# Three products of the RWKV-7 chain summed in one PSUM bank, with VectorE copying an operand out

## The chip, the core and the metric

The kernel runs on one core of a Trainium2 chip. The metric is the device time of one launch in microseconds (us), as a median of runs; lower is better. TensorE (PE) multiplies matrices into the eight banks of PSUM, VectorE (DVE) and ScalarE (ACT) read PSUM and SBUF, GpSimd (POOL) works on SBUF, and SyncE (SP) issues most transfers. Each of these takes its instructions strictly in the order in which they stand in its own queue.

## What is computed

One decoder layer over 1024 tokens of width 1024, in float32: an RMS norm, one wide input projection, three branches (RWKV-7 time mixing, a convolution module, cross-attention into 256 memory tokens), a gated merge, an output projection and a final norm. The change lies in the RWKV-7 branch. Its recurrence and the group norm behind it, cut from the reference:

```python
def step(state, inp):                       # per head; state is 64 x 64, all in float32
    r_t, w_t, k_t, v_t, a_t, b_t = inp
    sa = jnp.einsum('bhvk,bhk->bhv', state, a_t)
    state = (state * w_t[:, :, None, :]
             + sa[..., :, None] * b_t[:, :, None, :]
             + v_t[..., :, None] * k_t[:, :, None, :])
    y = jnp.einsum('bhvk,bhk->bhv', state, r_t)
    return state, y
_, ys = lax.scan(step, s0, seqs)            # 1024 steps, 16 heads
...
mu = jnp.mean(wkv, axis=-1, keepdims=True)
var = jnp.mean(jnp.square(wkv - mu), axis=-1, keepdims=True)
wkv = ((wkv - mu) * lax.rsqrt(var + RWKV_GN_EPS)).reshape(B, S, RWKV_WIDTH)
```

## The kernel before

**Stages.** Up to some 100 us the input is normalized and transposed. Up to some 1035 us the recurrence of the 16 heads runs between the matmuls of the input projection, and the rest of the time goes to the convolution, the attention and the output projections. Each float32 weight tile is split into two rounded parts, `wh` and `wl` (ACT casts, L123, DVE subtracts, L124), and each product of the projection is three matmuls of 128x512 into a bank `d` (L298, called dense matmuls here). 24 dense matmuls fill one bank.

**The chain.** A feature tile `j` (0 to 7) holds two heads, and the tokens come in two halves `e` (0 and 1). For each of these 16 pairs `g_chain` handles 8 chunks of 64 tokens in two groups `q` of 4, one chunk after the other, since each needs the state S that the one before left. The state of the two heads is a 128x128 tile, `s0[0]` and `s0[1]` in turn. `g` holds the masked products of all token pairs in a chunk, and `TT` the inverse of a triangular matrix that `g_sub` computes by substitution (31 steps of two small DVE instructions, L587 and L590, on tiles `W` and `U`).

- `g_pre` prepares a group: it transposes the keys into `tk` and the values into `sav`, multiplies `TT` into `tk` and `g`, and multiplies the part of `g` called AK with the values V (L666). AK V lands in the second half of a bank `tr` and ACT copies it to `Y` (L675).
- For each chunk PE multiplies `ar` by the state into a bank `ry` (L709). Half of the 128 rows of the result are the A S that the new operand needs, the other half are R S, a part of the output. DVE adds A S and the AK V in `Y` into `sav` (L710). PE multiplies `tk` by `sav` into a bank `sas` (L717), and two DVE instructions (L720), one for each head, turn that and ACT's scaled copy of the state (L713) into the next state.
- After four chunks PE multiplies `g` by `sav` into a bank `tr` (L731), ACT copies that to `Y` (L733), and two DVE instructions add the R S rows of `ry` (L738). Then come the statistics of the group norm (L742).
- After eight chunks, the tail of the chain: small DVE instructions, a reciprocal root on POOL (L114, L118), two DVE instructions over all of `Y` (L760, L761), and PE transposes `Y` into a bank `tr` (L766). DVE turns that into `o`, which SP stores to `o_rwkv_d` (L771).

**Banks.** PSUM's eight banks are `d` (2), `g` (2), `ry` (2), `sas` (1) and `tr` (1). The one bank `tr` serves the transposes of `g_pre`, AK V, the two products of `g_sub` that finish `TT` (L615 and L625, with ACT's copies `zt` and `TT` between, L619 and L629), the product of L731 and the transposes of the tail. Each user waits until the one before has been read.

**What sets the order.** The generators for dense work, `g_prep` (which makes `g`, `ar`, `bk`), `g_sub` and `g_chain` are mixed by shares of a step count in `mix`. From that the Tile framework's scheduler draws each engine's order, by its own estimates and by which banks and buffers are free in them, so an edit of the banks can move instructions on all engines. The order repeats with a period of one `j`, some 115 us: a chain for `e`=0, then one for `e`=1. Their two tails are called **tail 0** and **tail 1** here.

Of the kernel before, what the change touches and what calls it, by code (L numbers as in the profile page):

```python
# [13 lines left out]
ALU = mybir.AluOpType  # L14
# [4 lines left out]
P = 128  # L19
# [5 lines left out]
C = 64  # L25
# [7 lines left out]
RMS_EPS = 1e-6  # L33
LN_EPS = 1e-5
GN_EPS = 64e-5
PAIR_EVERY = 34.0
TAP = 1.4
LOS = (13, 14, 15, 16, 17)
# [24 lines left out]
def hybrid_kernel(ctx: ExitStack, tc: tile.TileContext, x: bass.AP, mem: bass.AP, wt: bass.AP,  # L63
# [272 lines left out]
    with tc.tile_pool(name="rk", bufs=1, reuse_waits="tile") as rk:  # L336
# [53 lines left out]
        def fl(ap):  # L390
            return ap.rearrange("p a t -> p (a t)")
# [240 lines left out]

        state = [0]

        def g_pre(j, e, q, g, bk, v, Y):
            tkp = bank("tr")
            for cc in range(4):
                pe.transpose(tkp[:, cc * P:(cc + 1) * P], fl(bk[:, q * 4 + cc, :, :]), ident)  # L640
            tk = rk.tile([P, 4, P], F32, name="tk", tag="tk", bufs=2)
            act.copy(tk, tkp.rearrange("p (c t) -> p c t", t=P))
            yield
            vtp = bank("tr")
            for cc in range(2):
                c = q * 4 + cc * 2
                pe.transpose(vtp[:, cc * P:(cc + 1) * P], v[:, c * C:(c + 2) * C], ident)
            sav = rk.tile([P, 4, P], F32, name="sav", tag="sav", bufs=2)
            for par in range(2):
                rows = slice(ko(par), ko(par) + C)  # L650
                act.copy(sav[rows, par::2, :], vtp[rows, 0:2 * P].rearrange("p (c t) -> p c t", t=P))
            yield
            zv = vtp[:, 2 * P:4 * P]
            u1 = bank("g", 2)
            uv = u1.rearrange("p (k c h t) -> p k c h t", k=2, c=2, h=2)
            for n in range(4):
                cc2, hh = n // 2, n % 2
                vsl = slice(hh * C, (hh + 1) * C)
                for par in range(2):
                    own = slice(so(par), so(par) + C)  # L660
                    oth = slice(ko(par), ko(par) + C)
                    cc = cc2 * 2 + par
                    gc = g[:, par, hh, q * 2 + cc2]
                    pe.matmul(uv[own, 0, cc2, hh, :], lhsT=TT[own, hh * 4 + q * 2 + cc2, :], rhs=tk[own, cc, vsl],
                              start=True, stop=True)
                    pe.matmul(zv[own, n * C:(n + 1) * C], lhsT=gc[oth, own], rhs=sav[oth, cc, vsl],  # L666
                              start=True, stop=True)
            for n in range(4):
                cc2, hh = n // 2, n % 2
                for par in range(2):  # L670
                    own = slice(so(par), so(par) + C)
                    oth = slice(ko(par), ko(par) + C)
                    pe.matmul(uv[own, 1, cc2, hh, :], lhsT=TT[own, hh * 4 + q * 2 + cc2, :],
                              rhs=g[own, par, hh, q * 2 + cc2, oth], start=True, stop=True)
            act.copy(fl(Y[:, q * 2:q * 2 + 2, :]), zv)  # L675
            for par in range(2):
                own = slice(so(par), so(par) + C)
                oth = slice(ko(par), ko(par) + C)
                act.copy(tk[own, par::2, :], uv[own, 0].rearrange("p c h t -> p c (h t)"))
                act.copy(g[own, par, :, q * 2:q * 2 + 2, oth], uv[own, 1].rearrange("p c h t -> p h c t"))  # L680
            yield (tk, sav)

        def g_chain(j, e):
            g, ar, bk, pc = GG.pop((j, e)), AR.pop((j, e)), BK.pop((j, e)), PCS.pop((j, e))
            v = VS.pop((j, e))
            if e == 0:
                dve.memset(s0[state[0]], 0.0)

            Y = rk.tile([P, 4, P], F32, name="Y", tag="Y", bufs=1)
            st = rk.tile([P, 4, 2, 6], F32, name="st", tag="st", bufs=1)  # L690
            pre = [g_pre(j, e, q, g, bk, v, Y) for q in range(2)]
            got = None
            for got in pre[0]:
                yield
# [2 lines left out]
            bv = rk.tile([P, HS], F32, name="bv", tag="bv", bufs=1)  # L697
            dve.tensor_tensor(out=bv, in0=bp, in1=v, op=ALU.mult)
            for q in range(2):
                tk, sav = got  # L700
                ry = bank("ry", 2)
                for cc in range(4):
                    c = q * 4 + cc
                    par = c % 2
                    cg = e * CPH + c
                    own = slice(so(par), so(par) + C)
                    cs = slice(cc * P, (cc + 1) * P)
                    S0, S1 = s0[state[0]], s0[1 - state[0]]
                    pe.matmul(ry[:, cs], lhsT=fl(ar[:, c, :, :]), rhs=S0, start=True, stop=True)  # L709
                    dve.tensor_tensor(out=sav[own, cc, :], in0=ry[own, cs], in1=Y[own, c // 2, :], op=ALU.add)  # L710
                    if cg < NCH - 1:
                        sp = rk.tile([P, P], F32, name="sp", tag="sp", bufs=1)
                        act.activation(sp, S0, AF.Copy, scale=pc[:, c:c + 1])  # L713
                    yield
                    if cg < NCH - 1:
                        sn = bank("sas")
                        pe.matmul(sn[:, 0:P], lhsT=tk[:, cc, :], rhs=sav[:, cc, :], start=True, stop=True)  # L717
                        for hh in range(2):
                            vsl = slice(hh * C, (hh + 1) * C)
                            dve.scalar_tensor_tensor(out=S1[vsl, vsl], in0=sn[vsl, vsl], scalar=pc[vsl, c:c + 1],  # L720
                                                     in1=sp[vsl, vsl], op0=ALU.mult, op1=ALU.add)
                        state[0] = 1 - state[0]
                    if q == 0 and cc < 3:
                        got = next(pre[1])
                    yield
                yp = bank("tr")
                for n in range(4):
                    cc2, hh = n // 2, n % 2
                    for par in range(2):
                        oth = slice(ko(par), ko(par) + C)  # L730
                        pe.matmul(yp[oth, n * C:(n + 1) * C], lhsT=g[:, par, hh, q * 2 + cc2, oth],  # L731
                                  rhs=sav[:, cc2 * 2 + par, hh * C:(hh + 1) * C], start=True, stop=True)
                act.copy(fl(Y[:, q * 2:q * 2 + 2, :]), yp[:, 0:2 * P])  # L733
                yield
                ryv = ry.rearrange("p (c t) -> p c t", t=P)
                for par in range(2):
                    oth = slice(ko(par), ko(par) + C)
                    dve.tensor_tensor(out=Y[oth, q * 2:q * 2 + 2, :], in0=Y[oth, q * 2:q * 2 + 2, :],  # L738
                                      in1=ryv[oth, par::2, :], op=ALU.add)
                for c2 in range(q * 2, q * 2 + 2):  # L740
                    for hh in range(2):
                        dve.bn_stats(out=st[:, c2, hh, :], in_=Y[:, c2, hh * C:(hh + 1) * C])  # L742
                yield
# [511 lines left out]
```

## Time and profile before

| what | value |
|---|---|
| median of 3 runs | 1951.31 us (1950.67 to 1953.14) |
| the profiled execution's own time | 1949.77 us |
| its span in the trace | 1947.8 us |
| PE busy over the span | 1844.5 us (95%) |
| DVE busy | 1410.6 us (72%) |
| ACT busy | 691.9 us (36%) |
| POOL busy | 227.7 us (12%) |
| mean granted TensorE clock | 0.993 of full speed |

PE is busy for 95% of the span, and the matmuls' number does not depend on the order, so the time is PE's work and PE's waits. "Busy" counts modelled ends of overlapping matmuls; a wait can thus be a little longer than the idle time that a row gives in brackets. The profile names for each idle stretch what released it. A wait of another engine matters where PE then waits for it.

### The profile page before, as it was taken

How to read it: one execution, taken by the hardware profiler on the slowest of the kernel's cores; microseconds unless marked ns; L12 is line 12 of the kernel's file. 1: busy time of each engine (PE TensorE's matmuls, PEld its weight loads, DVE VectorE, ACT ScalarE, POOL GpSimd, SP SyncE). 2: the span in 40 equal slices, each digit the busy share in tenths (PEclk: the TensorE clock that was granted, in tenths of full speed). 3: DMA queues.
4: the chain of work that ended last, by engine and by line, in shares of the span. 5: the costliest groups of instructions: out<-in, count | busy, mean ns of one | idle time of the engine just before them, and what ended most of it. 6: DMA issues, size and time to landing. Idle time of an engine off the chain costs nothing.

```text
span 1947.8 us, 30024 instructions
## 1 busy us (share of the span) xinstructions
PE 1844.5 (95%) x11412; PEld 1472.2 (76%) x11412; DVE 1410.6 (72%) x3028; ACT 691.9 (36%) x1303; POOL 227.7 (12%) x311
## 2 busy tenths in 40 slices
PE   6999998999899898998999999999999999899998
PEld 5777776766676676776788888888888788778886
DVE  5667787777878777787735998898999857654423
ACT  6334343433344343343333323131313335432121
POOL 2201111111111112111000000000000223100001
PEclk9999999999999999999999999999999999999999
DMA  4232212222121222212224411112122666785432
GB/s 147 57 99 58 77 35 63 60 56 74 42 83 44 62 63 53 77 42 71 69 72 141 130 54 55 65 59 71 44 76 87 227 199 214 246 283 170 129 130 86
DMA packets 127936, 188.61 MB, mean 97 GB/s; under 512 B 64432, under 2 KB 66608, under 8 KB 127792
## 3 DMA queue, kind: packets, MB, share of 16 engines
q1 hardware_dynamic: 122704, 178.11, 29.8%
q10 hardware_dynamic: 4768, 8.07, 1.1%
q8 instruction: 89, 1.46, 0.3%
q0 software_dynamic: 320, 0.52, 0.1%
q14 instruction: 55, 0.45, 0.1%
HBM read 139.92 MB, written 46.20 MB: 96 GB/s over the span
## 4 chain that ended last, share of the span: by engine, by line
PE 63%; DVE 23%; DMA 4%; issue 4%; ACT 3%; POOL 3%; SPq 0%; DVEq 0%; POOLq 0%; ACTq 0%
PE d L298 41%; PE g L298 5%; PE g L212 4%; DVE W L590 3%; DVE tm L587 3%; PE d L212 2%; DVE s L720 2%; PE g L552 2%; DVE wl L124 2%; DVE sav L710 1%; PE ry L894 1%; POOL vr L118 1%; DVE Y L761 1%; DVE Y L738 1%; PE sas L717 1%
## 5 line engine op out<-in xcount | busy, mean ns | idle before, releaser
L298 PE MATMUL d<-hH,wh 128*128 128x512 f32 x1504 | 607.2, 404 | 2.4 <-ACT lc L383 2.0
L298 PE MATMUL d<-hH,wl 128*128 128x512 f32 x1504 | 603.0, 401 | 0.0
L298 PE MATMUL d<-hL,wh 128*128 128x512 f32 x1504 | 600.1, 399 | 0.0
L298 PEld LDWEIGHTS d<-hH,wl 128*128 128x128 f32 x1504 | 285.0, 189 | 56.9
L298 PEld LDWEIGHTS d<-hH,wh 128*128 128x128 f32 x1504 | 285.3, 190 | 55.8 <-ACT lc L383 2.4
L298 PEld LDWEIGHTS d<-hL,wh 128*128 128x128 f32 x1504 | 285.0, 189 | 53.6
L848 DVE SCALAR_TENSOR_TENSOR ac<-up,wdw,ac 128x1024 f32<-128x1024 f32 x240 | 308.0, 1283 | 11.8 <-ACT ac L845 5.9
L123 ACT CAST wh<-wf 128x1024 fp32r<-128x1024 f32 x137 | 143.6, 1049 | 311.3 <-PE d L298 277.1
L124 DVE TENSOR_TENSOR wl<-wf,wh 128x1024 fp32r<-128x1024 f32 x137 | 177.6, 1296 | 83.8 <-ACT wh L123 83.3
L590 DVE TENSOR_TENSOR W<-W,tm 128x60 f32<-128x60 f32 (+24 forms) x496 | 112.3, 226 | 10.0
L587 DVE TENSOR_TENSOR tm<-W,U 128x60 f32<-128x60 f32 (+24 forms) x496 | 107.7, 217 | 11.1
L713 ACT ACTIVATE sp<-s,pc 128x128 f32<-128x128 f32 x120 | 48.3, 402 | 174.8 <-DVE s L720 137.6
L717 PEld LDWEIGHTS sas<-sav,tk 128*128 128x128 f32 x240 | 38.5, 188 | 67.7 <-DVE sav L710 49.4
L717 PE MATMUL sas<-sav,tk 128*128 128x128 f32 x240 | 54.2, 307 | 34.3 <-DVE sav L710 32.6
L720 DVE SCALAR_TENSOR_TENSOR s<-sas,pc,sp 64x64 f32<-64x64 f32 x240 | 67.6, 282 | 21.5 <-PE sas L717 16.1
L298 PE MATMUL g<-oH,wh 128*128 128x512 f32 x192 | 76.3, 398 | 5.3 <-ACT wh L123 5.3
L298 PE MATMUL g<-oH,wl 128*128 128x512 f32 x192 | 76.2, 397 | 2.1 <-DVE wl L124 2.1
L298 PE MATMUL g<-oL,wh 128*128 128x512 f32 x192 | 75.8, 395 | 0.0
L298 PE MATMUL d<-oL,wh 128*128 128x512 f32 x192 | 75.2, 392 | 0.0
L298 PE MATMUL d<-oH,wl 128*128 128x512 f32 x192 | 75.2, 392 | 0.0
L298 PE MATMUL d<-oH,wh 128*128 128x512 f32 x192 | 75.2, 392 | 0.0
L710 DVE TENSOR_TENSOR sav<-ry,Y 64x128 f32<-64x128 f32 x128 | 36.8, 287 | 43.7 <-ACT Y L675 26.8
(301 smaller groups left out, 2910.6 us busy)
## 6 DMA issues: line engine op xcount, KB each, us to landing
wf<-in_wt_dram SPq DMA_DIRECT2D x137, 512.0 KB
g_d<-gt SPq DMA_DIRECT2D x48, 256.0 KB
U<-ud SPq DMA_DIRECT2D x64, 128.0 KB
nxt<-in_x_dram SPq DMA_DIRECT2D x8, 512.0 KB
o_rwkv_d<-o SPq DMA_DIRECT2D x16, 256.0 KB
cv_d<-ac SPq DMA_DIRECT2D x8, 512.0 KB
o_mem_d<-om SPq DMA_DIRECT2D x16, 256.0 KB
xs<-cv_d SPq DMA_DIRECT2D x8, 512.0 KB
```

The costliest lines, as they stand in the source:

```text
L123: act.copy(hi, src)
L124: (eng or dve).tensor_tensor(out=lo, in0=src, in1=hi.bitcast(F32), op=ALU.subtract)
L212: pe.matmul(po, lhsT=l, rhs=r, start=(i == 0), stop=(i == n - 1))
L298: pe.matmul(po, lhsT=l[:, ks_], rhs=r[:, k, sl], start=(n == 0), stop=(n == 3 * KT - 1))
L552: pe.matmul(gps[hh][:, cc * P:(cc + 1) * P], lhsT=fl(bk[rows, c, :, :]), rhs=fl(ar[rows, c, :, :]), start=True, stop=True)
L587: dve.tensor_tensor(out=tv, in0=W[:, 0:m, i:i + 1].broadcast_to([NG * 32, m, n]), in1=U[:, i:i + 1, i + 1:32].broadcast_to([NG * 32, m, n] ...
L590: dve.tensor_tensor(out=wv_, in0=wv_, in1=tv, op=ALU.add)
L710: dve.tensor_tensor(out=sav[own, cc, :], in0=ry[own, cs], in1=Y[own, c // 2, :], op=ALU.add)
L713: act.activation(sp, S0, AF.Copy, scale=pc[:, c:c + 1])
L717: pe.matmul(sn[:, 0:P], lhsT=tk[:, cc, :], rhs=sav[:, cc, :], start=True, stop=True)
L720: dve.scalar_tensor_tensor(out=S1[vsl, vsl], in0=sn[vsl, vsl], scalar=pc[vsl, c:c + 1], in1=sp[vsl, vsl], op0=ALU.mult, op1=ALU.add)
L848: dve.scalar_tensor_tensor(out=ac, in0=up[:, tap:tap + S], scalar=wdw[:, tap * 8 + j:tap * 8 + j + 1], in1=ac, op0=ALU.mult, op1=ALU.add)
```

## The change

AK V is no longer written to a bank `tr` and copied to `Y`. Its matmuls write the `ry` bank of the group, which is now taken in `g_pre`; the first of them for each half of the rows starts the sums. The matmul of `ar` by the state adds to that (`start=False`), so that the rows of A S hold A S + AK V, and DVE copies them to `sav` with `tensor_copy` in place of the add. The product of `g` by `sav` is added onto the R S rows of the same bank, and two ACT copies of 64 rows take the sum to `Y`, in place of one ACT copy of 128 rows and two DVE adds. The manual dependencies only fix PE's own order. Nothing else is edited; the numbers of instructions on PE, ACT, POOL and SP stay the same, and DVE has 64 fewer. Cut to its core:

```diff
@@ g_pre
-            zv = vtp[:, 2 * P:4 * P]
+
+            ry = bank("ry", 2)
+            first = {}
             u1 = bank("g", 2)
...
-                    pe.matmul(zv[own, n * C:(n + 1) * C], lhsT=gc[oth, own], rhs=sav[oth, cc, vsl],
-                              start=True, stop=True)
+
+                    mm = pe.matmul(ry[own, cc * P + hh * C:cc * P + (hh + 1) * C], lhsT=gc[oth, own],
+                                   rhs=sav[oth, cc, vsl], start=par not in first, stop=False,
+                                   skip_group_check=True)
+                    if par in first:
+                        tc.add_manual_dep(mm.ins, first[par].name, NOSYNC, reason="sums begun in order")
+                    else:
+                        first[par] = mm.ins
...
-            act.copy(fl(Y[:, q * 2:q * 2 + 2, :]), zv)
...
-            yield (tk, sav)
+            yield (tk, sav, ry, first)
@@ g_chain
-                tk, sav = got
-                ry = bank("ry", 2)
+                tk, sav, ry, first = got
...
-                    pe.matmul(ry[:, cs], lhsT=fl(ar[:, c, :, :]), rhs=S0, start=True, stop=True)
-                    dve.tensor_tensor(out=sav[own, cc, :], in0=ry[own, cs], in1=Y[own, c // 2, :], op=ALU.add)
+                    mm = pe.matmul(ry[:, cs], lhsT=fl(ar[:, c, :, :]), rhs=S0, start=False, stop=False,
+                                   skip_group_check=True)
+                    for begun in first.values():
+                        tc.add_manual_dep(mm.ins, begun.name, NOSYNC, reason="sums begun in order")
+                    dve.tensor_copy(sav[own, cc, :], ry[own, cs])
...
-                yp = bank("tr")
                 for n in range(4):
                     cc2, hh = n // 2, n % 2
                     for par in range(2):
                         oth = slice(ko(par), ko(par) + C)
-                        pe.matmul(yp[oth, n * C:(n + 1) * C], lhsT=g[:, par, hh, q * 2 + cc2, oth],
-                                  rhs=sav[:, cc2 * 2 + par, hh * C:(hh + 1) * C], start=True, stop=True)
-                act.copy(fl(Y[:, q * 2:q * 2 + 2, :]), yp[:, 0:2 * P])
+                        cc = cc2 * 2 + par
+                        pe.matmul(ry[oth, cc * P + hh * C:cc * P + (hh + 1) * C],
+                                  lhsT=g[:, par, hh, q * 2 + cc2, oth], rhs=sav[:, cc, hh * C:(hh + 1) * C],
+                                  start=False, stop=True, skip_group_check=True)
                 yield
                 ryv = ry.rearrange("p (c t) -> p c t", t=P)
                 for par in range(2):
                     oth = slice(ko(par), ko(par) + C)
-                    dve.tensor_tensor(out=Y[oth, q * 2:q * 2 + 2, :], in0=Y[oth, q * 2:q * 2 + 2, :],
-                                      in1=ryv[oth, par::2, :], op=ALU.add)
+                    act.copy(Y[oth, q * 2:q * 2 + 2, :], ryv[oth, par::2, :])
```

The scheduler then gives all engines another order. Tail 0 on PE, before: L731 is the product of `g` by `sav`, and L625 the last product of `g_sub`, from which it takes over the one bank `tr`.

```order
L625 MATMUL tr<-zt,wb 32x32 x16
L298 MATMUL d<-hH,wh 128x512
L298 MATMUL d<-hL,wh 128x512
L298 MATMUL d<-hH,wl 128x512
L298 MATMUL d<-hH,wh 128x512
L731 MATMUL tr<-sav,g 64x64 x8
```

The same place in the changed kernel, from the last state product (`sas`) of the chain on:

```order
L727 MATMUL sas<-sav,tk 128x128
L299 MATMUL d<-hH,wh 128x512
L299 MATMUL d<-hL,wh 128x512
L299 MATMUL d<-hH,wl 128x512
L299 MATMUL d<-hH,wh 128x512
L741 MATMUL ry<-sav,g 64x64 x8
L299 MATMUL d<-hL,wh 128x512
L299 MATMUL d<-hH,wl 128x512
L616 MATMUL tr<-TT,g 32x32
```

The output product now stands ahead of both products of `g_sub` instead of behind them, 4 dense matmuls after the last state product.

Tail 1 on POOL, before: `U` is the operand of the next substitution, read back by a transfer, and `vr` the variance of the tail.

```order
L574 MEMSET W 128x256
L580 COPY W<-rb 32x8 x4
L581 TENSOR_TENSOR U<-U,rb 128x1024
L114 TENSOR_SCALAR vr<-vr 128x8
L118 TENSOR_TENSOR vr<-vr,nhalf 128x8
```

And in the changed kernel:

```order
L575 MEMSET W 128x256
L581 COPY W<-rb 32x8 x4
L115 TENSOR_SCALAR vr<-vr 128x8
L119 TENSOR_TENSOR vr<-vr,nhalf 128x8
L582 TENSOR_TENSOR U<-U,rb 128x1024
```

The multiplication of `U` has moved behind the root. In tail 0 it stood behind the root before, and does so still.

Tail 0 on SP, before, with `ud` the buffer in DRAM through which `U` is laid out anew:

```order
L560 DMA ud_414<-g 32x8x32 x4
L573 DMA U<-ud_414 32x1024 x4
L771 DMA o_rwkv_d_108<-o 128x512
L140 DMA wf<-in_wt_dram 128x1024
L437 DMA g_d_153<-gt 128x512
```

And in the changed kernel:

```order
L561 DMA ud_414<-g 32x8x32 x4
L574 DMA U<-ud_414 32x1024 x2
L780 DMA o_rwkv_d_108<-o 128x512
L574 DMA U<-ud_414 32x1024 x2
L141 DMA wf<-in_wt_dram 128x1024
```

Two of the four loads of `U` now stand behind the store of the tail's result `o`.

## Rows read from the trace of the kernel before

**Rows 1.** Windows: stretch, length, busy PE PEld DVE ACT POOL, clock, DMA share, GB/s.
```profile
100.00:1035.00 935.00, 867.26 (x6867) 664.40 (x6866) 691.04 (x2174) 360.01 (x767) 127.76 (x194) 0.99 0.23 63
```

**Rows 2.** Waits of PE, 100 to 1000 us: in total, times, longest.
```profile
PE sas L717 <- DVE sav L710: 32.6, 43, 1.9
PE tr L766 <- DVE Y L761: 19.1, 6, 3.2
PE tr L766 <- DVE W L590: 6.2, 6, 1.0
PE ry L709 <- DVE s L720: 5.8, 13, 0.9
```

**Rows 3.** Timeline of PE: start, us, what, in brackets idle before and releaser.
```profile
409.87 0.69 PE L731 MATMUL tr<-sav,g 128*64 128x64 f32 x16
...
419.61 0.63 PE L766 MATMUL tr<-ident,Y 128*128 128x128 f32 x4 [3.16 <-DVE Y L761]
...
479.25 0.63 PE L766 MATMUL tr<-ident,Y 128*128 128x128 f32 x4 [1.03 <-DVE W L590]
...
535.01 0.63 PE L766 MATMUL tr<-ident,Y 128*128 128x128 f32 x4 [3.16 <-DVE Y L761]
...
1720.83 0.68 PE L298 MATMUL g<-oH,wh 128*128 128x512 f32 x1 [1.92 <-ACT wh L123]
```

**Rows 4.** Windows: around tail 0, at the same place a period later, and at 1720.8 us.
```profile
410.80:416.10 5.30, 5.30 (x25) 4.32 (x23) 4.43 (x15) 1.72 (x3) 1.62 (x2) 1.00 0.36 99
419.60:424.00 4.40, 4.39 (x18) 3.68 (x19) 1.50 (x2) 1.18 (x2) 0.00 (x0) 0.61 0.31 79
535.00:539.40 4.40, 4.39 (x50) 3.58 (x52) 1.50 (x2) 1.81 (x4) 0.00 (x0) 1.00 0.39 83
1720.80:1724.00 3.20, 2.79 (x6) 1.78 (x7) 2.66 (x4) 0.69 (x2) 0.00 (x0) 0.53 0.76 269
```

**Rows 5.** Timeline of ACT, DVE and POOL in tail 0.
```profile
410.60 0.37 ACT L733 COPY Y<-tr 128x256 f32<-128x256 f32 x1 [1.00 <-PE tr L731]
411.01 0.85 DVE L738 TENSOR_TENSOR Y<-Y,ry 64x256 f32<-64x256 f32 x2 [2.93 <-ACT Y L733]
...
412.94 1.22 DVE L124 TENSOR_TENSOR wl<-wf,wh 128x1024 fp32r<-128x1024 f32 x1
...
414.97 1.64 POOL L118 TENSOR_TENSOR vr<-vr,nhalf 128x8 f32<-128x8 f32 x1
416.58 2.34 POOL L581 TENSOR_TENSOR U<-U,rb 128x1024 f32<-128x1024 f32 x1
416.65 2.82 DVE L761 TENSOR_TENSOR Y<-Y,vr 128x512 f32<-128x512 f32 x1 [1.09 <-POOL vr L118]
```

**Rows 6.** Timeline of SP, POOL and DVE in tail 1.
```profile
464.81 1.76 SPq L573 DMA_DIRECT2D U<-ud  x4
...
469.09 2.39 POOL L581 TENSOR_TENSOR U<-U,rb 128x1024 f32<-128x1024 f32 x1 [5.99 <-DMA U<-ud]
...
478.41 0.69 DVE L761 TENSOR_TENSOR Y<-Y,vr 128x512 f32<-128x512 f32 x1 [1.94 <-POOL vr L118]
```

**Rows 7.** Timeline of DVE and ACT ahead of tail 0's last product.
```profile
405.24 0.90 DVE L607 STREAM_TRANSPOSE TT<-wb 32x256 f32<-32x256 f32 x2 [1.00 <-DMA wb<-wd]
...
406.92 0.74 ACT L619 COPY zt<-tr 32x256 f32<-32x256 f32 x2 [3.59 <-PE tr L615]
```

**Rows 8.** Groups by line and shape: count, busy us, mean ns, idle before, releaser.
```profile
L710 DVE TENSOR_TENSOR sav<-ry,Y 64x128 f32<-64x128 f32 x128 | 36.8, 287 | 43.7 <-ACT Y L675 26.8 <-PE ry L709 13.9
...
L738 DVE TENSOR_TENSOR Y<-Y,ry 64x256 f32<-64x256 f32 x64 | 26.8, 419 | 34.6 <-ACT Y L733 33.7
...
L1028 DVE COPY vt<-sas 128x8 f32<-128x8 f32 x1 | 0.2, 159 | 0.0
...
L651 ACT COPY sav<-tr 64x256 f32<-64x256 f32 x64 | 23.3, 365 | 18.6 <-PE tr L647 18.2
...
L733 ACT COPY Y<-tr 128x256 f32<-128x256 f32 x32 | 11.7, 364 | 16.5 <-PE tr L731 16.4
```

More of the change, by code (lines that the diff above doesn't have):

```diff
@@ L35 @@
 GN_EPS = 64e-5
+NOSYNC = mybir.DependencyInfo(mybir.DependencyClass.NoSync, mybir.DependencyReason.DATA)
 PAIR_EVERY = 34.0
@@ L635, in hybrid_kernel, with g_pre @@
         state = [0]
-        def g_pre(j, e, q, g, bk, v, Y):
+        def g_pre(j, e, q, g, bk, v):
             tkp = bank("tr")
@@ L690, in g_chain @@
             st = rk.tile([P, 4, 2, 6], F32, name="st", tag="st", bufs=1)
-            pre = [g_pre(j, e, q, g, bk, v, Y) for q in range(2)]
+            pre = [g_pre(j, e, q, g, bk, v) for q in range(2)]
             got = None
```

## The prediction

> **What bounds the kernel now.** I read the page first, which shows PE busy throughout, then the windows by stage. While the chain runs, from 100 to 1035 us, PE is busy for 867.3 of 935.0 us and DVE for 691.0 [rows 1]; after that PE hardly waits and nothing is changed. So the change is worth what it does to the 68 us that PE stands idle there. The waits of PE [rows 2] split them: 32.6 us before the state product for the operand `sav`, 5.8 us before the product with the state, and 25.3 us before the transposes of a finished chain, in twelve places. The timeline shows what these twelve are [rows 3]: tail 0 of a period costs 3.16 us (six times, 19.1 us together) and tail 1 costs 1.03 us (six times, 6.2 us). [...]
>
> **Tail 0, the output product moved.** Before, it waited for the bank `tr` and stood behind `g_sub`'s two products; 25 dense matmuls then covered the path to the transposes. They step by 0.22 us (24 of them in 5.30 us [rows 4]), and with the product's own 0.69 us [rows 3] they cover 6.2 us of the 9.7 us from 409.87 to 419.61 [rows 3]. In the order of the changed kernel the product comes earlier: ahead of the transposes stand itself (0.65), 20 dense matmuls (4.4), both products of `g_sub` and eight of `g_prep`, three blocks that I put at the output product's 0.69 each (2.1), 7.1 us in all. The path behind it also changes. ACT starts 0.73 us after the product (409.87 to 410.60) and makes two copies of 64 rows, 0.37 us each [rows 5, 8], in place of one. From the first add (411.01) to the root (414.97) there were 3.96 us [rows 5]; the adds' 0.85 go, the weight's low part (1.22) now stands behind, and two transposes of 0.45 [rows 7] come between: 2.8. The root takes 1.64, and DVE's last pass 0.69 where nothing stops it [rows 6]. With 0.2 for the hand-overs that is 0.73 + 0.74 + 2.8 + 1.64 + 0.69 + 0.2 = 6.8 us, less than 7.1, to which the waits of the next paragraph add. So the six waits go: **-19.1**, and with them the five lost clocks: **-8.5**.
>
> The same move costs something. `g_sub`'s first product needs transposes that wait for a transfer (1.00 us of waiting already [rows 7]), and only six dense matmuls and the output product, 2.0 us, stand between the last state product and it, where there were twelve dense matmuls, 2.6 us. I take 0.7 us of new wait, with a few tenths for the hand-over 0.8. Its second product needs ACT's copies `zt`, 0.74 us [rows 7], and only four products of `g_prep` (half a block, 0.35 us) stand between: 0.5. Seven periods: **+9**, between 0 (if the transfer comes earlier, since the substitution ends earlier) and +14.
>
> **Tail 1.** Its path is the same 6.8 us, begun some 0.4 us later because DVE's transposes for `g_sub` stand ahead of the statistics; PE has 20 dense matmuls, itself and two blocks, 6.5 us, and waits some 0.6 us for `g_sub`'s operands. Left is a wait of 0.1 to 0.3. With 0.6 for the operands that is 0.9 where 1.03 stood: **0**.
>
> But POOL's order has changed here: `U` now comes behind the root, as it did in tail 0. There the multiplication of `U` ran from 416.58 to 418.92, and DVE's last pass, begun at 416.65, took 2.82 us [rows 5] in place of 0.69 [rows 6]: 2.1 us more. [...] So what counts is whether `U` has landed when the root ends. Its loads were issued from 464.81 to 466.57 and it started on POOL at 469.09 [rows 6], 2.5 us later. In the changed order SP has two stores to `ud` between the loads of the transposes and those of `U`, but the substitution ends some 2 us earlier. I put the landing at 469 again. Between the last product with the state and the output product stood 42 dense matmuls and two blocks, now 12 dense: 30 x 0.22 + 1.4 = 8.0 us less. The root ended at 478.4 (DVE's pass waited for it [rows 6]), so it now ends near 470.4, with DVE's half microsecond near 471: after the landing, by 1 to 2 us. So DVE's pass is stopped, and in seven periods that is 7 x 2.1 = **+14.7**. A wait of 2.4 us then stands before tail 1's transposes. Of shorter waits than 3.16 one of 1.9 us left the clock at 0.53 [rows 3, 4]; I count two lost clocks of seven, **+3.4**.
>
> **The operand.** The add of 64x128 took 287 ns, 128 times [rows 8]. A copy out of PSUM of that size is not in the trace. Nearest below is a copy of 8 columns, 159 ns, and nearest above the add itself [rows 8]. At the add's rate, (287 - 159) / 120 or 1.07 ns a column, the copy would be 284 ns; I take that, since the shape is the add's: 128 x 3 ns is nothing, and at most 128 x 128 ns = 16 us of DVE's time.
>
> [...]
>
> **The chain.** The 64 adds of 419 ns that go [rows 8] are 26.8 us of DVE's 691, but in the new order four or five pairs of the substitution stand where they stood, so the operand behind them is hardly earlier. ACT gets 64 copies of 365 ns for 32 of 364 [rows 8] and loses the 32 copies of AK V, which is even. The waits for `sav` and the state are 38.4 us [rows 2]. In 12 places two dense matmuls or none stood between the product with the state and the state product; now it is four or more everywhere, two to four more of 0.22 us as cover: 12 x 0.6 = 7 us. Another 3 us for DVE's shorter queue: **-10**, between -20 and +5.
>
> **Sum.** Own time 1949.8 - 19.1 - 8.5 + 9 + 0 + 14.7 + 3.4 - 10 = 1939.3. The profiled run is 1.5 us below the median of the runs, so 1941 us.
>
> **Rivals.**
> - *`U` comes too late to stop tail 1.* Then the last two plus terms fall away: 1941 - 18 = 1923 us. For it: the margin is 1 to 2 us, and SP's queue has two more stores ahead of `U`. Against: in tail 0 this order of POOL stopped DVE in all six waits [rows 2].
> - *`U` comes too late for the substitution* (slower). At tail 0 two of `U`'s four loads stand behind the store of `o`, and ahead of `o` on DVE now stand a weight's part (1.22 [rows 5]) and three passes of some 0.7: the store comes some 3.5 us after the transposes. With two issues (half of 1.76), the landing (2.5 [rows 6]) and POOL's 2.34 `U` is done 9.2 us after the transposes. DVE's first substitution step stands behind the first state update, which stands behind 26 matmuls of 128x512 (5.7 us), four blocks of `g_pre` (2.8) and the update's own way over DVE (some 1.5): 10 us. So there is 0.8 us of slack. From there on DVE stands still, with the next operands behind it, and PE pays in seven periods: the gain of 10 us is eaten when `U` is 0.8 + 1.5 us late, and at 4 us late it is 7 x 3.2 = 22 us more, 1963 us.
> - *Nothing moves*: the tight places of the new order cost what the old ones did, and the waits taken from the tails come up before `sav`, DVE being at 74%: 1951 us. For it: DVE's idle time in the tails was also where it caught up.
>
> **How the numbers follow.** Forecast (tail 0 free, tail 1 stopped) 0.50; tail 1 free 0.27; nothing moves 0.12; `U` late 0.11. The range takes the forecast's bounds (-14 to +14), the first rival's 1923 less a few, and ends just above no change: 1917 to 1953. About 0.2% (3.9 us) is what a measurement here can tell from no change. Faster by that: the first rival and nine tenths of the forecast, 0.72; slower: `U` late and a little, 0.12; the rest 0.16.
>
> **What would show it.** In the changed trace: tail 0's transposes without a wait and the clock at 1.00 behind them; new waits of 0.5 to 1 us before `g_sub`'s two products; POOL's `U` beginning where the root ends in tail 1 and DVE's last pass at 2.8 us there; copies to `sav` at 260 to 285 ns; the waits for `sav` below 32.6 us. If tail 0 still waits over 1 us, the path was mis-summed; if the stage's idle time shrinks by less than 5 us with the tails free, the chain took it back.

## The result, and the profile after

| | kernel before | changed kernel |
|---|---|---|
| median | 1952.22 us of 4 runs (1950.67 to 1953.48) | 1939.68 us of 4 runs (1935.22 to 1941.39) |
| ratio | 1 | 0.9932, 95% interval 0.992 to 0.9945 |
| the profiled execution, own time and span | 1949.77, 1947.8 us | 1935.22, 1933.3 us |

The change takes 0.7% off, 12.5 us between the medians. The forecast was 1941 us, 0.9947 of the median it started from. As the terms below show, the total is closer than its parts.

The stage windows of the changed kernel (stretch, length, busy PE, PEld, DVE, ACT, POOL, clock, DMA share, GB/s) answer to [rows 1] and, for two stretches of lower clock, to [rows 4]:

```profile
100.00:1035.00 935.00, 871.80 (x6930) 671.80 (x6928) 678.25 (x2114) 370.82 (x775) 126.82 (x198) 0.99 0.24 67
425.00:430.00 5.00, 4.13 (x14) 3.48 (x15) 3.66 (x18) 1.14 (x3) 0.00 (x0) 0.66 0.00 0
760.00:765.00 5.00, 3.85 (x11) 3.17 (x12) 3.94 (x18) 1.14 (x3) 0.24 (x1) 0.53 0.00 0
```

PE's idle time in this stretch shrank by only 4.5 us (67.7 to 63.2), but more matmuls fit into it: 6930 in place of 6867. The waits of PE over the same stretch (waiting and awaited instruction: us in all, times, longest) answer to [rows 2]:

```profile
PE sas L727 <- DVE sav L720: 44.7, 46, 2.0
PE tr L775 <- DVE Y L770: 12.1, 7, 1.9
PE ry L716 <- DVE s L730: 4.3, 15, 0.7
PE tr L626 <- ACT zt L620: 1.1, 6, 0.2
```

Before the transposes PE now waits 12.1 us in seven places, where it was 25.3 in twelve; [rows 2] end at 1000 us, and up to 1035 us the kernel before has two more of these waits, 1.8 us, at the last tails. Before the state product, for `sav`, it waits 12.1 us more than before. The timeline of PE (start, us, instruction, idle before and releaser) shows the tails, as [rows 3] did: tail 0's product and its transposes, then two tails 1.

```profile
288.15 0.69 PE L741 MATMUL ry<-sav,g 128*64 128x64 f32 x16
...
297.25 0.60 PE L775 MATMUL tr<-ident,Y 128*128 128x128 f32 x4
...
354.72 0.63 PE L775 MATMUL tr<-ident,Y 128*128 128x128 f32 x4 [1.89 <-DVE Y L770]
...
465.95 0.60 PE L775 MATMUL tr<-ident,Y 128*128 128x128 f32 x4
```

Tail 0 never waits, in eight of eight. Tail 1 waits 1.88 to 1.90 us in six of the seven that have a `U` beside them, and at 465.95 not at all. The timeline of POOL and DVE in these two tails tells why, and answers to [rows 5, 6]:

```profile
351.65 2.37 POOL L582 TENSOR_TENSOR U<-U,rb 128x1024 f32<-128x1024 f32 x1
351.72 2.85 DVE L770 TENSOR_TENSOR Y<-Y,vr 128x512 f32<-128x512 f32 x1 [2.12 <-POOL vr L119]
...
465.00 0.69 DVE L770 TENSOR_TENSOR Y<-Y,vr 128x512 f32<-128x512 f32 x1 [2.12 <-POOL vr L119]
465.07 2.88 POOL L582 TENSOR_TENSOR U<-U,rb 128x1024 f32<-128x1024 f32 x1
```

At 351.65 `U` starts 0.07 us ahead of the last pass over `Y`, and the pass takes 2.85 us. At 465.00 the pass starts 0.07 us ahead: it takes 0.69, and `U` takes 2.88 in place of 2.37. In both tails the one that starts first runs at its own length and the other is held: the pass ends 0.55 us after `U` (354.57 and 354.02) in the first, `U` 2.26 us after the pass (467.95 and 465.69) in the second, a little less than each takes where nothing holds it.

The group of DVE that answers to [rows 8] (count, busy us, mean ns, idle before):

```profile
L720 DVE COPY sav<-ry 64x128 f32<-64x128 f32 x128 | 36.8, 287 | 19.3 <-PE ry L716 16.4
```

The copy takes 287 ns, to the nanosecond what the add took, and the prediction's 284 ns was near. A copy in place of the add gives DVE no time: 36.8 us for the 128 of them, before and after.

### The profile page after: what moved, and what is told of

The parts are those of the page before. It is cut to its first block, busy times and chain, and to the rows that moved or that the text cites. A ratio compares the mean times of both kernels' runs of the same rounds, so it can differ in the third digit from the quotient of the medians.

```text
span 1933.3 us, 29922 instructions
## 1 busy us (share of the span) xinstructions
PE 1834.4 (95%) x11412; PEld 1467.6 (76%) x11412; DVE 1390.4 (72%) x2964; ACT 697.6 (36%) x1303; POOL 226.5 (12%) x311
## 4 chain that ended last, share of the span: by engine, by line
PE 64%; DVE 24%; issue 4%; DMA 3%; ACT 3%; POOL 2%; SPq 0%; DVEq 0%; POOLq 0%; ACTq 0%
PE d L299 42%; PE g L299 5%; PE g L213 4%; DVE tm L588 4%; DVE W L591 4%; PE d L213 2%; DVE s L730 2%; PE g L553 2%; DVE wl L125 1%; DVE sav L720 1%; PE ry L903 1%; PE sas L727 1%; DMA xv<-cv_d 1%; PE ry L213 1%; DVE Y L770 1%
## 5 line engine op out<-in xcount | busy, mean ns | idle before, releaser
L857 DVE SCALAR_TENSOR_TENSOR ac<-up,wdw,ac 128x1024 f32<-128x1024 f32 x240 | 307.4, 1281 | 11.8 <-ACT ac L854 6.0
L125 DVE TENSOR_TENSOR wl<-wf,wh 128x1024 fp32r<-128x1024 f32 x137 | 168.6, 1231 | 61.9 <-ACT wh L124 61.6
L727 PEld LDWEIGHTS sas<-sav,tk 128*128 128x128 f32 x240 | 39.1, 190 | 80.4 <-DVE sav L720 63.2
L727 PE MATMUL sas<-sav,tk 128*128 128x128 f32 x240 | 54.3, 308 | 45.7 <-DVE sav L720 44.7
L864 POOL TENSOR_TENSOR csum<-csum,ac 128x1024 f32<-128x1024 f32 x7 | 19.6, 2796 | 388.6 <-DVE ac L857 388.6
```

Source lines behind the costliest of these rows:

```text
L125: (eng or dve).tensor_tensor(out=lo, in0=src, in1=hi.bitcast(F32), op=ALU.subtract)
L857: dve.scalar_tensor_tensor(out=ac, in0=up[:, tap:tap + S], scalar=wdw[:, tap * 8 + j:tap * 8 + j + 1], in1=ac, op0=ALU.mult, op1=ALU.add)
L864: pool.tensor_tensor(out=csum, in0=csum, in1=ac, op=ALU.add)
```

## The experiments

Three questions were open. Which half of the change moves the time? Is it the place of the output product or the shorter path behind it? And what does `U` cost, in tail 1 and elsewhere? Each kernel was timed against the kernel before, whose median was 1952.22 us beside the changed kernel, 1949.42 beside the first four kernels below and 1948.47 beside the last four. So kernels of different groups are best compared by their ratios; where only medians are compared, it is said.

### One half alone: the output product

```diff
@@ g_chain of the kernel before
-                    pe.matmul(ry[:, cs], lhsT=fl(ar[:, c, :, :]), rhs=S0, start=True, stop=True)
+                    pe.matmul(ry[:, cs], lhsT=fl(ar[:, c, :, :]), rhs=S0, start=cc == 0, stop=False,
+                              skip_group_check=True)
...
-                yp = bank("tr")
...
+                        pe.matmul(ry[oth, cc * P + hh * C:cc * P + (hh + 1) * C],
+                                  lhsT=g[:, par, hh, q * 2 + cc2, oth], rhs=sav[:, cc, hh * C:(hh + 1) * C],
+                                  start=False, stop=True, skip_group_check=True)
...
-                    dve.tensor_tensor(out=Y[oth, q * 2:q * 2 + 2, :], in0=Y[oth, q * 2:q * 2 + 2, :],
-                                      in1=ryv[oth, par::2, :], op=ALU.add)
+                    act.copy(Y[oth, q * 2:q * 2 + 2, :], ryv[oth, par::2, :])
```

> One part alone: the output product is added onto R S and two ACT copies take the sum to Y; AK V, its copy to Y and DVE's add for the operand stay as before. The order of every engine is that of the changed kernel but for the AK V instructions themselves. Theory M (the gain comes from the output product leaving the bank tr, which lets it stand ahead of the substitution's products): tail 0 without a wait, tail 1 stopped by U at 1.9 us, 1936 to 1945 us, ratio 0.993 to 0.997. Theory V (the gain comes from AK V leaving tr, whose users then wait less in short waits that the profile counts as busy, 13 us in all): 1948 to 1954 us, ratio 0.998 to 1.001, with the blocks of g_pre as long as before.

Measured: 1938.60 us, ratio 0.9945 (0.9928 to 0.9961). Theory M holds: the ratio is that of the changed kernel (0.9932) within the intervals, and the waits of PE are, within 3 us:

```profile
PE sas L718 <- DVE sav L711: 47.3, 48, 2.0
PE tr L766 <- DVE Y L761: 12.3, 7, 2.1
```

### The other half alone: AK V and the copy

```diff
@@ g_chain of the changed kernel
-                        pe.matmul(ry[oth, cc * P + hh * C:cc * P + (hh + 1) * C],
-                                  lhsT=g[:, par, hh, q * 2 + cc2, oth], rhs=sav[:, cc, hh * C:(hh + 1) * C],
-                                  start=False, stop=True, skip_group_check=True)
+                yp = bank("tr")
...
+                        pe.matmul(yp[oth, n * C:(n + 1) * C], lhsT=g[:, par, hh, q * 2 + cc2, oth],
+                                  rhs=sav[:, cc2 * 2 + par, hh * C:(hh + 1) * C], start=True, stop=True)
+                act.copy(fl(Y[:, q * 2:q * 2 + 2, :]), yp[:, 0:2 * P])
...
-                    act.copy(Y[oth, q * 2:q * 2 + 2, :], ryv[oth, par::2, :])
+                    dve.tensor_tensor(out=Y[oth, q * 2:q * 2 + 2, :], in0=Y[oth, q * 2:q * 2 + 2, :],
+                                      in1=ryv[oth, par::2, :], op=ALU.add)
```

> The other part alone: AK V is summed in ry and DVE copies the operand; the output product stays in the bank tr, with an ACT copy and two DVE adds. Theory M: the output product stands behind the substitution's products again, with 25 dense matmuls behind it as before, so tail 0's wait of some 3 us and its lost clock are back: 1944 to 1953 us. Theory V: 13 us of short waits go here: 1936 to 1941 us.

Measured: 1969.86 us, ratio 1.0107 (1.0092 to 1.0121). Both theories missed: it is 20 us slower than before. Two of its waits, two places of the timeline in a tail 0 and a tail 1, and a window behind the first of them (columns as above):

```profile
PE tr L776 <- DVE Y L771: 33.3, 9, 4.0
PE sas L727 <- DVE sav L720: 28.7, 40, 1.8
```

```profile
309.58 1.09 PE L776 MATMUL tr<-ident,Y 128*128 128x128 f32 x4 [3.96 <-DVE Y L771]
...
372.01 0.30 PE L776 MATMUL tr<-ident,Y 128*128 128x128 f32 x1 [3.96 <-DVE Y L771]
```

```profile
310.00:315.00 5.00, 5.00 (x17) 4.08 (x16) 1.99 (x5) 0.59 (x1) 0.00 (x0) 0.50 0.28 105
```

The output product stands behind the substitution's products again, and here `U` follows the root not only in the tails 0 but also in three of the tails 1, so nine tails wait 3.2 to 4.0 us. Behind the first, five whole microseconds ran at 0.50. Summed over windows of 5 us (length times what the clock lacks to 1), this execution lost 18.6 us to the clock and the profiled one of before 8.5. With 8 us more of waiting in the tails, 2.4 more for the state and 3.9 less for `sav`, that is 16.6 of the 22.8 us between the spans.

### The move undone

```diff
@@ g_sub of the changed kernel, behind its last product
+            zlast[2 * j + e] = mm.ins
+            behind(2 * j + e)
@@ g_chain, at the output product
+                        if q == 1 and e == 0:
+                            yfirst.setdefault(2 * j + e + 1, []).append(mm.ins)
...
+        def behind(n):
+            if n in zlast and n in yfirst:
+                for mm in yfirst[n]:
+                    tc.add_manual_dep(mm, zlast[n].name, NOSYNC, reason="output product behind the substitution's")
```

> The changed kernel with the move undone in tail 0 alone: the output product is held behind the last product of the substitution, still in ry and without DVE adds; the sums and the instructions are those of the changed kernel. 16 dense matmuls (3.6 us) and the product's own 0.7 are left ahead of the transposes, and the path behind the product is 6.5 to 7.0 us. Theory M: tail 0 waits 2 to 4.5 us again in seven periods, with lost clocks, 16 to 35 us above the changed kernel: 1953 to 1972 us. Rival (tail 0 is free because two DVE adds went from its path, wherever the product stands): under 1 us of wait, 1936 to 1945 us.

Measured: 1953.87 us, ratio 1.002 (1.0006 to 1.0034), 17 us above the changed kernel by the ratios (14 between the medians). PE's waits before the transposes, and the place in tail 0 that answers to 288.15 and 297.25 above:

```profile
PE tr L788 <- DVE Y L783: 25.2, 14, 3.5
```

```profile
294.17 0.69 PE L750 MATMUL ry<-sav,g 128*64 128x64 f32 x16
...
300.74 0.63 PE L788 MATMUL tr<-ident,Y 128*128 128x128 f32 x4 [1.61 <-DVE Y L783]
```

The time is in theory M's range; the wait, 1.6 us in six tails 0, is below its 2 to 4.5 and above the rival's 1. The waits before the transposes are 13.1 us more than in the changed kernel. (The profiled execution took 1947.27 us, 6.6 below the median.) So with less cover behind the product the wait comes back, and with it the time.

The experiment does not separate the product's place from the shorter path, though. It leaves 16 dense matmuls behind the product, where the kernel before had 25. Those 25 covered 6.6 us (409.87 to 419.61 less the wait of 3.16 [rows 3]), and the path measured here is 6.6 us as well (294.17 to 300.74). So at the old place, with 25 behind it, the shorter path might just have been covered; no such kernel was run.

The wait is also only half of the 3.16 us of [rows 3], which left a question: what was the other half? In this kernel the last pass takes 0.69 us in tail 0. Before it took 2.82 [rows 5].

### One POOL instruction between the root and U, after the change and before it

```diff
@@ g_chain, in the changed kernel and in the kernel before
             rsqrt(vr, vr, 1.0 / C, GN_EPS)
+            gap = rk.tile([P, n2], F32, name="gap", tag="gap", bufs=1)
+            pool.tensor_copy(gap, vr)
```

The copy needs the root's result, as the last pass does, and `U` doesn't. So the copy was put between them to keep `U` from starting ahead of the pass.

> The changed kernel with one more POOL instruction, a copy of 128x8 (0.2 us) between the root and U's multiplication; no other instruction moves. It gives DVE's last pass over Y the start ahead of U. Theory P (U's multiplication, begun 0.07 us ahead of the pass, holds it for 2.2 us): the pass takes 0.69 us in all 16 tails, PE's waits before the transposes fall from 12.1 us to under 2, the lost clocks behind them go, 1924 to 1931 us. Rival (the chain takes it back: the same microseconds come up before sav, since DVE is the bound there): tails free, waits for sav above 50 us, 1936 to 1941 us. Rival (the pass is long for another reason): 2.85 us as before, 1936 to 1941 us.

Measured: 1917.94 us, ratio 0.9843 (0.983 to 0.9856): 17 us less than the changed kernel by the ratios, 22 between the medians. The pass takes 0.69 us in all 16 tails. Its waits, and POOL and DVE in the tail 1 that answers to 351.65 above:

```profile
PE sas L727 <- DVE sav L720: 47.2, 48, 2.0
...
PE tr L777 <- DVE Y L772: 0.8, 1, 0.8
```

```profile
350.63 0.69 DVE L772 TENSOR_TENSOR Y<-Y,vr 128x512 f32<-128x512 f32 x1 [2.12 <-POOL vr L119]
...
350.66 0.71 POOL L767 COPY gap<-vr 128x8 f32<-128x8 f32 x1
...
351.33 2.39 POOL L582 TENSOR_TENSOR U<-U,rb 128x1024 f32<-128x1024 f32 x1
```

DVE now starts 0.03 us ahead, and it is POOL's copy that is held: it takes 0.71 us, where the root's first instruction on POOL (L115, 128x8 as well) took 0.20 two microseconds earlier. The tails' waits fell by 11.3 us and the clock's loss from 11.8 to 1.7; 2.5 us came up before `sav`. Theory P's mechanism holds, and the time is below its range.

> The kernel before with the same POOL copy of 128x8 between the root and U's multiplication; nothing else moves, and nothing of the change is in it. Theory P (what tail 0 lost was the start that U has on the last pass): the pass falls from 2.82 to 0.69 us in the six tails 0, PE's wait there from 3.16 to 1.0 us, the lost clocks behind it go: 6 x 2.1 + 8.5 = 21 us less than before, 1926 to 1933 us, ratio 0.988 to 0.992. Rival (the chain takes it back before sav): 1940 to 1950 us.

Measured: 1928.86 us, ratio 0.99 (0.9882 to 0.9918), as theory P has it. Waits, and the tail that answers to 419.61 in [rows 3] and to [rows 5]:

```profile
PE sas L717 <- DVE sav L710: 31.5, 42, 1.5
...
PE tr L768 <- DVE Y L763: 6.4, 6, 1.1
```

```profile
415.78 0.69 DVE L763 TENSOR_TENSOR Y<-Y,vr 128x512 f32<-128x512 f32 x1 [1.10 <-POOL vr L118]
415.81 0.71 POOL L758 COPY gap<-vr 128x8 f32<-128x8 f32 x1
416.48 2.38 POOL L581 TENSOR_TENSOR U<-U,rb 128x1024 f32<-128x1024 f32 x1
...
416.61 0.30 PE L768 MATMUL tr<-ident,Y 128*128 128x128 f32 x1 [1.04 <-DVE Y L763]
```

So 2.1 of tail 0's 3.16 us were `U`'s hold, and from 100 to 1035 us no window of 5 us in this execution is below 0.97 of the clock; from 416.6 to 421, behind the wait of 1.04, it reads 1.00. One POOL instruction, with nothing of the change, takes more off (20 us) than the change does (12.5). Together they take 31.

### The output product alone, with the gap

The two edits above together, on the kernel before.

> The output product alone in ry (AK V, its copy and DVE's add as before) with the POOL copy behind the root; the order is that of e3_gap but for AK V's own instructions. Theory M (AK V's part of the change and the copy in place of the add are worth nothing): within 0.2% of e3_gap, 1914 to 1922 us. Rival (once the tails are free, ACT's 32 copies and the bank tr count): 1924 to 1930 us.

Measured: 1918.91 us, ratio 0.9849 (0.983 to 0.9869), 0.06% from e3_gap. Theory M holds with the tails free too.

### U's hold on the next chain

In tail 0 the changed kernel has two of `U`'s loads behind the store of `o`, so `U` now lands at the start of the next chain. The timeline of the changed kernel there:

```profile
305.16 2.39 POOL L582 TENSOR_TENSOR U<-U,rb 128x1024 f32<-128x1024 f32 x1 [10.74 <-DMA U<-ud]
...
306.10 1.73 DVE L488 TENSOR_SCALAR lw<-lw 128x512 f32<-128x512 f32 x1
...
307.86 0.29 DVE L720 COPY sav<-ry 64x128 f32<-64x128 f32 x1
...
308.20 0.38 PE L727 MATMUL sas<-sav,tk 128*128 128x128 f32 x1 [1.27 <-DVE sav L720]
```

L488 takes 0.43 us elsewhere. Here it ends at 307.83, just after `U` (307.55); the operand's copy stands behind it, and PE waits 1.27 us.

```diff
@@ g_prep, with the gap
-            dve.tensor_scalar(out=lw, in0=lw, scalar1=1.0, scalar2=-0.5 * DECAY_C, op0=ALU.add, op1=ALU.mult)
+            act.activation(lw, lw, AF.Copy, scale=-0.5 * DECAY_C, bias=-0.5 * DECAY_C)
```

> e3_gap with one DVE instruction of the preparation (the scaling of lw, 128x512) on ACT instead; 20 lines of PE's order differ. In the trace it took 1.2 to 2.4 us in place of 0.43 in five periods, while U was multiplied, with the first operand of a chain behind it. Theory C (PE's new waits for sav at the start of tail 0's successor are U's hold on DVE): the wait of 1.3 us before that chain's first state product goes, 6 to 12 us less than e3_gap: 1905 to 1913 us, waits for sav from 47 to 40 us or less. Rival (the next instruction of DVE with two SBUF inputs, the scan, is held in its place, and the second operand waits behind it): 1914 to 1920 us.

Measured: 1914.01 us, ratio 0.9818 (0.9801 to 0.9835), the lowest time of the study, 22 us below the changed kernel by the ratios (25.7 between the medians). Below `e3_gap` it is 5 us by the ratios and 3.9 between the medians, at the border of the two ranges, and the intervals overlap: the time does not decide. The waits for `sav` in all, then two state products of `e3_gap`, then POOL, DVE and PE of this kernel at the same place:

```profile
PE sas L727 <- DVE sav L720: 40.5, 42, 2.8
```

```profile
307.06 0.49 PE L727 MATMUL sas<-sav,tk 128*128 128x128 f32 x2 [1.25 <-DVE sav L720]
...
312.46 0.49 PE L727 MATMUL sas<-sav,tk 128*128 128x128 f32 x2 [1.24 <-DVE sav L720]
```

```profile
301.32 2.39 POOL L582 TENSOR_TENSOR U<-U,rb 128x1024 f32<-128x1024 f32 x1 [9.94 <-DMA U<-ud]
...
302.32 0.29 DVE L720 COPY sav<-ry 64x128 f32<-64x128 f32 x1
...
302.71 1.55 DVE L125 TENSOR_TENSOR hsl<-kk,hsh 128x512 fp32r<-128x512 f32 x1
...
309.24 0.49 PE L727 MATMUL sas<-sav,tk 128*128 128x128 f32 x2 [2.08 <-DVE sav L720]
```

The copy out of PSUM runs beside `U` unheld (0.29 us, as elsewhere), and the first state product no longer waits. The next instruction with two SBUF inputs is held in L488's place (1.55 in place of 0.69), as the rival said, though it is L125 and not the scan, and the second state product waits 2.08 us in place of 1.24. Over the seven periods the first of these waits went from 6.7 us to nothing and the second grew from 10.2 to 16.0, so the waits at this place fell by only 0.9 us. The total fell by the 6.7 us that theory C forecast, but that is luck: 4.0 of them went before the fifth state product of the chain ahead of tail 0 and 2.0 before the fourth of the chain behind it, where no `U` runs. Why was not traced. And the clock lost 6.75 us in this execution, against 1.7 in that of `e3_gap`.

### U's multiplication cut to the columns that are read

```diff
@@ g_sub, with the gap
-            pool.tensor_tensor(out=U, in0=U, in1=rb[:, None, :].broadcast_to([NG * 32, 32, 32]), op=ALU.mult)
+            for r_, n in ((0, 32), (8, 24), (16, 16)):
+                k_ = 16 if r_ == 16 else 8
+                uq = U[:, r_:r_ + k_, 32 - n:32]
+                pool.tensor_tensor(out=uq, in0=uq, in1=rb[:, None, 32 - n:32].broadcast_to([NG * 32, k_, n]),
+                                   op=ALU.mult)
```

> e3_gap with U's multiplication in three pieces that leave out the columns the substitution never reads, 640 of 1024, the result unchanged: POOL some 1.6 us in place of 2.4, no piece over 0.7. The scheduler moves the tails' products by a few places on PE. Theory C: the holds on DVE shrink, 1903 to 1915 us. Rival (the other order of PE costs as much as the shorter hold gains): 1916 to 1930 us.

Measured: 1922.65 us, ratio 0.9866 (0.985 to 0.9883), in the rival's range and 4.7 us above e3_gap between the medians, though the intervals touch. The three pieces hold 704 of the 1024 columns, not 640, and took 2.0 us together in tail 1, not 1.6. The pass is free, but the new order costs: tail 1's product stands behind the first of `g_sub`'s products, no longer ahead of both. What follows it, 20 dense matmuls and one product of `g_sub`, covers 6.3 us, where `e3_gap` has 7.4, and the transposes wait.

```profile
455.17 0.68 PE L745 MATMUL ry<-sav,g 128*64 128x64 f32 x14
...
462.88 0.30 PE L781 MATMUL tr<-ident,Y 128*128 128x128 f32 x1 [1.39 <-DVE Y L776]
```

## Why the prediction was right, and where its terms were not

The case that was put first is the one that came: tail 0 free in eight of eight, tail 1 stopped by `U` in six of seven. Neither `U` rival came: `U` reached tail 1's root in time to stop the pass, and where it landed late, at 305.16, it was done 3 us before the substitution's first step. The median was 1.3 us off, but most terms were far off and cancelled: that the total came so near is luck. Of the prediction's own signs, the free tail 0, `U` beginning at the root and the pass at 2.8 us came; the new waits before `g_sub`'s products (0.18 us), the copies at 260 to 285 ns (287) and the waits for `sav` below 32.6 us (44.7) did not. The stage's idle time shrank by 4.5 us, less than the 5 at which the prediction would say that the chain took it back, and in part the chain did. The measured column is the profiled execution of the changed kernel against that of before.

| step | predicted, us | measured, us |
|---|---|---|
| tail 0's six waits | -19.1 | -19.1 |
| the clock, tails 0 and 1 together | -8.5 + 3.4 = -5.1 | +3.3 |
| new waits before `g_sub`'s products | +9 | +1.1 |
| tail 1 | 0 + 14.7 | 12.1 - 6.2 = +5.9 |
| the chain's waits (`sav`, state) | -10 | +12.1 - 1.5 = +10.6 |
| short waits inside PE's small products | none | -13 |
| two waits at the last tails | none | -1.8 |
| sum | -10.5 | -13.0, against 14.5 between the spans |

**Tail 0.** The path was put at 6.8 us and took 7.0 (288.15 to 295.14, the pass's end); the cover was put at 7.1 and was 9.1 (288.15 to 297.25), since the three blocks took 3.4 us in place of 2.1 and the 20 dense matmuls 5.1 in place of 4.4. That the tail came free was right, and the kernel that holds the product back shows that the wait returns with less cover. But the path has the last pass at 0.69 us without a reason, although `U` stands behind the root here too; it came out so because `U` landed only at 305.16. With a hold of 2.1 us the path would have been 9.1, no less than the cover. What the prediction did not say either is that 2.1 of the 3.16 us were `U`'s hold, which the step had in hand in [rows 5] and used for tail 1 alone.

**Tail 1.** The stop came as it had in tail 0 of the kernel before: `U` 0.07 us ahead there (416.58 and 416.65 [rows 5]) and 0.07 ahead here, the pass 2.82 us there and 2.85 here. The term was too large: it put the hold on top of a tail that would wait 0.9 us in any case, 0.6 of it for `g_sub`'s operands. That wait wasn't there, and of the hold's 2.16 us (2.85 - 0.69) PE's cover took 0.27, so that 1.89 were left where 1.03 had stood.

**`g_sub`'s products.** The step failed on how the order was read. Only the first matmul of the first product stands early; the other 15 have six dense matmuls more. Of the waits before both products one of 0.18 us is left in six periods (L626 above).

**The clock.** The sum takes a lost clock at 1.7 us, five times and twice. The trace of before shows 1.5 to 1.7 us lost behind five of tail 0's six waits (4.4 us at 0.61 four times and at 0.65 once) and none behind the sixth (1.00), so the size came near, and the five at tail 0 went. But six others came where the sum has two: three behind waits of 1.93 to 2.02 us for `sav` (the two windows above are among them), three behind tail 1's 1.89. There the 5 us from the wait's end read 0.50 once and 0.66 to 0.67 five times, and behind the other three of tail 1's waits 1.00. The waits alone did not set the loss: the kernel with the output product alone has those of the changed one within 3 us, and its profiled execution lost 3.4 us to the clock where the changed kernel's lost 11.8. Whether differences of this kind are why the changed kernel's runs spread over 6 us and those of e3_gap, whose tails don't wait, over 3 was not shown: the changed kernel's run of 1935.22 us had a mean clock of 0.991, and the one of 1938.34 us had 0.993.

**The chain.** Here the step failed. It counted on 12 places with two dense matmuls or none between the product with the state and the state product. Those are the second and third state products of the chain ahead of tail 0, in six periods, and none of the 43 waits of [rows 2] lies there, so that more cover had nothing to shorten. The waits grew instead, from 32.6 to 44.7 us, and the first two state products of the chain behind tail 0 make up that growth: 3.8 us before, 15.7 after. (The other places rise and fall by as much.) Ahead of the first of them now stand four dense matmuls and little else, where in six periods seven or eight and the products of `g_pre` stood. And `U` now runs there in all seven periods and holds DVE: L488 in five, and in the other two the scan behind it, which takes 1.23 us elsewhere.

```profile
418.20 2.40 POOL L582 TENSOR_TENSOR U<-U,rb 128x1024 f32<-128x1024 f32 x1 [12.00 <-DMA U<-ud]
...
418.71 2.96 DVE L494 TENSOR_TENSOR_SCAN lw<-rmask,lw 128x512 f32<-128x512 f32 x1
...
425.87 0.79 PE L727 MATMUL sas<-sav,tk 128*128 128x128 f32 x2 [2.02 <-DVE sav L720]
```

`U`'s new place at the start of a chain was seen in SP's order and weighed only for the substitution. How much of the 11.9 us is `U`'s hold and how much the new order stays open: no run of the new order left DVE free there, and with `U` in three shorter pieces, which held L488 in one period only (0.87 us), this place still waited 14.9 us.

**What the sum lacked.** PE's idle time hardly shrank, so most of the gain lies in time that counts as busy. From the start of each run of small products to the next dense matmul, with the listed waits taken off, the stretch from the first tail 0 (183 us) to the last (975.6 after, 989.5 before) holds 211.1 us before, 198.2 after, 196.9 with the output product alone and 214.5 with AK V alone. In the same stretch, which shrank by 13.3 us, the dense matmuls took 532.9 us before and 535.4 after, and the waits 61.8 and 59.0, so nearly all of the shrinking lies in the small products. One such place of the kernel before, on PE and on ACT, and the same place after, on PE:

```profile
308.57 0.39 PE L647 MATMUL tr<-ident,v 128*128 128x128 f32 x2
...
309.79 0.51 PE L666 MATMUL tr<-sav,g 64*64 64x64 f32 x10
...
310.46 0.50 PE L480 MATMUL g<-lox,wuH 128*128 128x512 f32 x1
```

```profile
308.99 0.74 ACT L651 COPY sav<-tr 64x256 f32<-64x256 f32 x2 [0.25 <-PE tr L647]
```

```profile
300.21 0.38 PE L649 MATMUL tr<-ident,v 128*128 128x128 f32 x2
300.35 0.48 PE L299 MATMUL d<-hH,wh 128*128 128x512 f32 x1
...
301.22 0.27 PE L668 MATMUL g<-tk,TT 64*64 64x64 f32 x1
```

Before, the products of `g_pre` follow the transposes of V directly, and AK V starts at 309.79, 0.06 us after ACT has copied V (308.99 + 0.74). No row calls that a wait, since the ends of the matmuls ahead of it are modelled. In PE's order there are 13 places of 32 with no dense matmul between, and with AK V alone 13 again; in the changed kernel and with the output product alone there is none, and two or more stand everywhere. With the product held back there are 6, and the sum is 200.5. The sums fall with the counts; that these places are all of the 13 us was not tested.

## What to carry to other kernels

When two engines can hold each other, look at who starts first: here 0.07 us decided over 2.2 us, and one cheap instruction that waits for the same result turned it round, for 20 us. When an edit moves an instruction to another time, ask what it can hold there, and not only who waits for its result. When a total of waits falls as forecast, look where it fell before calling the cause shown: with L488 moved, 6.7 us went, and only 0.9 of them at the place in question. And cut a change in its halves before crediting both: one half here had the whole gain, the other nothing, or a loss of 20 us when it stood alone.

## What the runs showed of the hardware

- `U`'s multiplication on POOL and instructions of DVE made each other longer, whichever came second: the last pass took 2.85 us in place of 0.69 where `U` had started 0.07 us ahead, `U` took 2.88 in place of 2.37 where the pass had, and POOL's copy `gap`, begun 0.03 us behind the pass, took 0.71.
- Beside `U`, a DVE TENSOR_SCALAR of 128x512 in float32 with one tensor input (L488) took 1.20 to 2.38 us in five places in place of 0.43, where the kernel before had one such place (2.40), and a scan of 128x512 with two inputs from SBUF took 2.96 and 2.99 in place of 1.23. A copy of 64x128 out of PSUM took 0.29 us there, as elsewhere.
- A DVE copy of 64x128 out of PSUM took as long as an add of PSUM and SBUF of that size, 287 ns as the mean of 128 each.
- TensorE's granted clock read 0.66 in the 5 us behind three of tail 1's six waits of 1.88 to 1.90 us and 1.00 behind the other three; behind three waits of 1.93 to 2.02 us for `sav` it read 0.50 to 0.67. Two executions with waits within 3 us of each other lost 3.4 and 11.8 us to it.
